# MLP of a two-layer encoder: more pairs with seven products, sums of the chunks added by DMAs, residual kept in DRAM meanwhile

## The chip, the cores and the metric

The kernel runs on one core of a Trainium2 chip. The metric is the device time of one execution in microseconds (us). The profile is one execution taken by the hardware profiler. Its engines are named PE (matrix multiplies; PEld is the load of the stationary operand, which overlaps PE), DVE (elementwise on two inputs), ACT (copies, casts, functions), POOL (elementwise, and here also an issuer of DMAs) and SP (issues DMAs only).

## The reference

256 tokens with 2048 features pass through two layers. Each layer has attention (layer 0: a chunked softmax; layer 1: stick-breaking) beside a cross-attention of four heads into 256 memory tokens, and then an MLP with 8192 hidden features. Only this part of it, and where the residual `h` is read, matter here:

```python
def sq_relu_mlp(h, g, w_in, w_out):
    return jnp.square(jax.nn.relu(rms_norm(h, g) @ w_in)) @ w_out
...
    for layer in range(DEPTH):          # DEPTH = 2
        ...
        h = h + jnp.concatenate([y_main, y_mem], axis=-1) @ w_o[layer]
        h = h + sq_relu_mlp(h, norm_mlp[layer], w_mlp_in[layer], w_mlp_out[layer])
```

Everything is float32.

## The kernel before

**Precision.** Each float32 operand is split into `hi` (a cast to the fp32r type) and `lo = x - hi`, and a product is three matmuls: hi·hi, hi·lo, lo·hi. A weight unit is 128x1024 values. SP loads it into a tile `raw` (6 buffers), ACT casts it to `hi` (4 buffers), DVE subtracts to get `lo` (5 buffers). `weights()` hands the units out in the order of a list, `stream`, and has the units after the one it hands out prepared, up to four.

**MLP.** The 8192 hidden features are four chunks `c` of 2048, and a chunk is 16 tiles `f` of 128 features. A step U computes one tile: 16 matmuls of 128x512 with the `hi` of two weight units, then 16 of 128x256 with their `lo`. Its result leaves PSUM in `up`: ACT copies one half (`low`, L449), DVE adds the other (L1174), DVE applies relu and the norm (L1156), ACT squares (L1159), and the tile is split into `hid` (L1114, L1115).

The second projection takes the tiles of a chunk in eight pairs `j`, tiles 2j and 2j+1. Its 2048 outputs are two halves `n` of 1024. For one pair and one half, tokens, features and outputs are a 2x2 by 2x2 product of blocks. It is done in one of two ways:

- directly, in two steps A and B, with one weight unit each and 12 matmuls of 128x512 each, together 24;
- with seven products instead of eight, in one step S (`seven`): 21 matmuls, from four weight units that here are called W0 to W3. W0 holds two blocks as they were loaded, W1 one block (128x512), W2 and W3 two each that DVE makes from the raw blocks in place, by four subtractions and additions of 128x512 (L220, L221 for W2; L223, L224 for W3; each needs the one before). The step uses them in this order with 6, 3, 6 and 6 matmuls. On the other side, `block_sums` makes the sums and differences of the pair's tiles, `s_w` and `s_x` (four DVE operations of 128x128, L1137 to L1140, and the splits). They serve both halves n of a chunk.

`SEVEN = 5`: pairs 0 to 4 go by S, 5 to 7 by A and B. In the last chunk only half 0 goes this way; half 1 is done plainly at the end.

**Order of the work.** `TURNS` writes out one turn per chunk and half, and `mlp_steps` reads it, both for `stream` and for the program. PE executes exactly in this order. In half 0 the turn makes the remaining U of the same chunk, in half 1 the first U of the next one. The `up` of a tile is written in the program where its U ends; the preparation of W2 and W3 of a following S is written behind it, since `weights()` looks four units ahead. The other engines' instructions are put in order by a scheduler when the kernel is built; from then on the order on each engine is fixed.

**Sums.** A turn accumulates eight PSUM banks: four outputs `11`, `21`, `12`, `22` and four products `p1`, `p5`, `p6`, `p7` that enter more than one output. `add` brings a finished bank into SBUF sums (`d`: four tiles, `e`: three, 128x1024 each). In chunk 0 these are mostly ACT copies (L1080), in later chunks DVE adds from PSUM (L1082), of which `p1` takes two. At the end `merged` adds the products into the outputs (L1027), and `turned` transposes the sums and adds them to `h` (L1011).

**Buffers.** Tiles of 128x1024 come from the pool `grp` with 13 buffers. During an MLP these hold four tiles of `h`, four `d`, three `e`, and the keys and values of the memory for layer 1.

Of the kernel before, what the change touches and what calls it, by code (L numbers as in the profile page):

```python
# [16 lines left out]
P = 128  # L17
# [28 lines left out]
SEVEN = 5  # L46
ALONE = 10
TURNS = (
    "U10 S0 U11 S1 U12 A5 S2 U13 S3 U14 A6 S4 U15 B5 B6 A7 B7",
    "U0 S0 U1 A5 U2 S1 U3 A6 U4 S2 U5 A7 U6 S3 U7 S4 U8 B5 U9 B6 B7",  # L50
)


def mlp_steps():

    steps = [(0, 0, "H", 0)] + [(0, 0, "T", f) for f in range(FIRST_UP, ALONE, 2)]
    for c in range(NCH):
        for n in range(2 if c < NCH - 1 else 1):
            for step in TURNS[n].split():
                kind, i = step[0], int(step[1:])  # L60
                steps.append((c + 1 if kind == "U" and n == 1 else c, n, kind, i))
    return steps
# [41 lines left out]
def trunk(  # L104
# [27 lines left out]
    tiny = ctx.enter_context(tc.tile_pool(name="tiny", bufs=4))  # L132
    ps_mm = ctx.enter_context(tc.tile_pool(name="ps_mm", bufs=4, space=PSUM))
# [132 lines left out]
    def start_side(g):  # L266
        active.append(g)
# [302 lines left out]
    def normed_heads(banks, eps_ms, gain, dst, wait=2):  # L570
# [24 lines left out]
        def side():  # L595
# [3 lines left out]
            for m in range(2):  # L599
# [11 lines left out]
                )  # L611

# [11 lines left out]
    def heads4(name):  # L624
        return grp.tile([P, 1024], F32, name=name, tag="g4")

# [190 lines left out]
    def mlp_stream(l):  # L817
# [5 lines left out]
        for c, n, kind, i in mlp_steps():  # L823
# [115 lines left out]
    km, vm = [], []  # L939

    for l, mg in enumerate((mg0, mg1)):
# [10 lines left out]
        def keys(b, wait, k_=k_, g=g):  # L952

            late = 2 + wait
            later(lambda: normed_heads(b, mstat["em"], sm[:, g : g + 1], k_[:], late), wait)
# [10 lines left out]
        else:  # L966
            tokens_major(mg, lambda b: keys(b, 0))
            tokens_major(mg, lambda b: value_heads(b, mstat["r"], vm[1]))
# [16 lines left out]
    def mlp(l, xg_, sq, h, done):  # L985
# [7 lines left out]
        extra = [heads4(f"e{l}_{i}") for i in range(3)]  # L993

        def product_sum(i, n):

            return extra[i][:, n * 512 : (n + 1) * 512]
# [18 lines left out]
        def merged(n):  # L1016

            u, p5, p7 = (product_sum(i, n) for i in range(3))
            for i, (dst, src) in enumerate((
                (summed(0, 2 * n + 1), u),  # L1020
                (summed(0, 2 * n + 1), p5),
                (u, p7),
                (summed(1, 2 * n), u),
                (u, p5),
                (summed(1, 2 * n + 1), u),
            )):
                pin(nc.vector.tensor_tensor(dst, dst, src, op=ALU.add))  # L1027
# [10 lines left out]
        sevens = SEVEN  # L1038

        class Group:  # L1040

            def __init__(self, c, n, factors, staged=None):
                self.c, self.factors, self.staged = c, factors, staged
# [387 lines left out]
```

## Time and profile before

| | us |
|---|---|
| runs | 2158.01, 2158.10, 2158.83 (median 2158.1) |
| profiled execution | 2158.02 |
| its span, first to last instruction | 2156.3 |
| busy: PE / DVE / ACT / POOL | 2148.9 / 1745.1 / 1248.3 / 205.5 |
| layer 0, chunk 1, half 0 | about 665 to 739 of the span |
| layer 0, chunk 1, half 1 | about 739 to 834 of the span |

Busy time is the time in which at least one instruction of the engine ran, and neighbours overlap a little; so the time that an instruction takes up in a full queue is the distance from its start to the next start, somewhat less than its own duration. "Waits" name who waited for whom. Names have their buffer numbers left out: `acc` is any PSUM accumulator. POOL issues no DMA in this kernel.

### The profile page before, as it was taken

What the parts mean: (1) busy time and instruction counts of PE and PEld (TensorE: products, weight loads), DVE (VectorE), ACT (ScalarE), POOL (GpSimd) and SP (SyncE); (2) the same over time, 40 slices, a digit from 0 to 9 for tenths busy, and PEclk for the clock granted to TensorE, in tenths of its full rate; (3) what the DMA queues carried; (4) which work ended last, traced back from release to release, by engine and by line L of the source; (5) the groups of instructions that cost most, each with busy time, mean ns of one, the idle gap of its engine ahead of it and who ended that gap; (6) DMA issues with size and microseconds to landing.
All of it is one profiled execution on the core that took longest, in us unless ns stands there. A gap on an engine that the chain in (4) does not pass through costs nothing.

```text
span 2156.3 us, 30341 instructions
## 1 busy us (share of the span) xinstructions
PE 2148.9 (100%) x11038; PEld 1841.2 (85%) x11038; DVE 1745.1 (81%) x2603; ACT 1248.3 (58%) x1828; POOL 205.5 (10%) x223
## 2 busy tenths in 40 slices
PE   9999999999999999999999999999999999999999
PEld 8888888888888888888888889888888888888887
DVE  7778885679898899989986556566988888988995
ACT  7744545556666566566555547655666656556663
POOL 0010112610000000000050112252000000000000
PEclk9999999999999999999999999999999999999999
DMA  9655556656666756666766654455666666666674
GB/s 331 193 165 187 167 180 195 196 188 187 192 200 200 214 180 197 205 199 196 215 177 194 187 187 137 131 184 184 185 214 186 197 205 200 202 194 205 186 224 128
DMA packets 213317, 414.65 MB, mean 192 GB/s; under 512 B 13232, under 2 KB 144304, under 8 KB 213168
## 3 DMA queue, kind: packets, MB, share of 16 engines
q1 hardware_dynamic: 212592, 410.63, 62.0%
q8 instruction: 86, 1.41, 0.3%
q10 hardware_dynamic: 576, 2.10, 0.3%
q14 instruction: 63, 0.52, 0.1%
HBM read 410.58 MB, written 2.10 MB: 191 GB/s over the span
## 4 chain that ended last, share of the span: by engine, by line
PE 98%; DVE 2%; issue 0%; ACT 0%; DVEq 0%
PE acc L75 93%; PE accs L75 1%; PE yp L75 1%; PE tp L75 1%; PE s L75 1%; PE z L75 1%; DVE lo L226 0%; PE cold L75 0%; DVE lo L174 0%; DVE pt L654 0%; DVE lo L248 0%; ACT hi L171 0%; DVE h L1011 0%; PE stat L75 0%; DVE raw L223 0%
## 5 line engine op out<-in xcount | busy, mean ns | idle before, releaser
L174 DVE TENSOR_TENSOR lo<-raw,hi 128x1024 fp32r<-128x1024 f32 (+1 forms) x524 | 642.5, 1237 | 220.9 <-ACT hi L171 194.8
L171 ACT CAST hi<-raw 128x1024 fp32r<-128x1024 f32 (+1 forms) x524 | 539.2, 1045 | 339.2 <-PE acc L75 286.0
L75 PE MATMUL acc<-mlpx,hi 128*128 128x512 f32 x2048 | 483.9, 389 | 0.0
L75 PE MATMUL acc<-hi,hid 128*128 128x512 f32 x1404 | 474.4, 391 | 0.0
L75 PEld LDWEIGHTS acc<-mlpx,hi 128*128 128x128 f32 x2048 | 383.6, 188 | 79.3
L225 ACT CAST hi<-raw 128x1024 fp32r<-128x1024 f32 (+1 forms) x280 | 264.8, 946 | 204.9 <-DVE raw L221 132.8
L226 DVE TENSOR_TENSOR lo<-raw,hi 128x1024 fp32r<-128x1024 f32 (+1 forms) x280 | 302.0, 1087 | 34.6 <-ACT hi L225 29.5
L75 PEld LDWEIGHTS acc<-hi,hid 128*128 128x128 f32 x1404 | 264.0, 188 | 52.6
L75 PE MATMUL acc<-lo,hid 128*128 128x512 f32 x702 | 274.5, 391 | 0.0
L75 PEld LDWEIGHTS acc<-mlpx,lo 128*128 128x128 f32 x2048 | 261.3, 191 | 9.0
L75 PE MATMUL acc<-mlpx,lo 128*128 128x256 f32 x2048 | 264.6, 283 | 0.0
L75 PE MATMUL acc<-hi,xg 128*128 128x512 f32 x640 | 208.4, 398 | 0.0
L75 PEld LDWEIGHTS acc<-lo,hid 128*128 128x128 f32 x702 | 132.3, 188 | 23.2
L247 ACT CAST hi<-raw 128x1024 fp32r<-128x1024 f32 x108 | 113.4, 1055 | 65.2 <-PE acc L75 54.6
L449 ACT COPY low<-acc 128x256 f32<-128x256 f32 x188 | 69.4, 369 | 136.1 <-PE acc L75 135.0
L75 PEld LDWEIGHTS acc<-hi,xg 128*128 128x128 f32 x640 | 120.2, 188 | 24.6
L248 DVE TENSOR_TENSOR lo<-raw,hi 128x1024 fp32r<-128x1024 f32 x108 | 131.0, 1230 | 6.1 <-ACT hi L247 6.1
L75 PE MATMUL acc<-lo,xg 128*128 128x512 f32 x320 | 124.7, 390 | 0.7 <-DVE lo L174 0.7
L75 PE MATMUL acc<-y,hi 128*128 128x512 f32 x512 | 119.9, 391 | 0.0
L75 PEld LDWEIGHTS acc<-y,hi 128*128 128x128 f32 x512 | 95.0, 188 | 19.1
L75 PE MATMUL acc<-hi,s_w 128*128 128x512 f32 x280 | 97.6, 389 | 0.0
L1159 ACT ACTIVATE up<-up 128x256 f32<-128x256 f32 x128 | 52.8, 415 | 40.2 <-DVE up L1156 40.2
(211 smaller groups left out, 2612.6 us busy)
## 6 DMA issues: line engine op xcount, KB each, us to landing
raw<-in_w_up SPq DMA_DIRECT2D x256, 512.0 KB, 4.8
raw<-in_w_down SPq DMA_DIRECT2D x256, 512.0 KB, 6.0
raw<-in_w_in SPq DMA_DIRECT2D x80, 512.0 KB, 3.9
raw<-in_w_o SPq DMA_DIRECT2D x64, 512.0 KB, 4.2
raw<-in_w_mem SPq DMA_DIRECT2D x28, 512.0 KB, 5.8
raw<-in_w_kv_v SPq DMA_DIRECT2D x24, 512.0 KB, 4.1
raw<-in_w_kv_k SPq DMA_DIRECT2D x24, 512.0 KB, 4.4
raw<-in_w_q SPq DMA_DIRECT2D x24, 512.0 KB, 4.2
```

What stands on the lines that cost most here:

```text
L75: return self._tc.keep_in_program_order(fn(*args, **kwargs))
L171: nc.scalar.copy(hi[:, :n], raw[:, :n])
L174: nc.vector.tensor_tensor(lo, raw, hi.bitcast(F32), op=ALU.subtract)
L225: nc.scalar.copy(hi4, src)
L226: nc.vector.tensor_tensor(lo4, src, hi4.bitcast(F32), op=ALU.subtract)
L247: nc.scalar.copy(hi4, turned)
L248: nc.vector.tensor_tensor(lo4, turned, hi4.bitcast(F32), op=ALU.subtract)
L449: nc.scalar.copy(low[:], bank[:, T:])
L1159: nc.scalar.activation(a[:], a[:], AF.Square)
```

## The change

The number of pairs that go by S is set by chunk: 7, 7, 6 and 5 of 8 in chunks 0 to 3, in both layers (it was 5 in each). There are new turns for 5, 6 and 7 pairs, and `ALONE` goes from 10 to 9: half 1 of a chunk makes nine U of the next, half 0 the other seven.

The bank of each output or product has one home now, so there are four `e` tiles instead of three, and `p1` is added once; `merged` makes up for it with eight adds instead of six. In chunk 0 all eight banks are copied by ACT. In chunks 1 and 2 ACT copies each bank into a half of a fresh 128x1024 tile `copy`, and when both halves are there POOL issues a DMA that adds the tile to its home in SBUF (`accum_op=ALU.add`). In chunk 3 DVE adds as before.

To make room, POOL issues DMAs that write the four tiles of `h` to DRAM as they are finished before an MLP (`put_away`) and bring them back in its last chunk (`bring_back`), and do the same with the memory keys and values of layer 1 between their computation and their use. In chunks 0 and 1 the `s_w` and `s_x` of pair 6 share a tile of `grp`.

```diff
-SEVEN = 5
-ALONE = 10
-TURNS = (
-    "U10 S0 U11 S1 U12 A5 S2 U13 S3 U14 A6 S4 U15 B5 B6 A7 B7",
-    "U0 S0 U1 A5 U2 S1 U3 A6 U4 S2 U5 A7 U6 S3 U7 S4 U8 B5 U9 B6 B7",
-)
+SEVEN = [[7, 7, 6, 5], [7, 7, 6, 5]]
+ALONE = 9
+TURNS = {
+    5: (
+        "U S0 U S1 U S2 U A5 U S3 U A6 S4 U B5 B6 A7 B7",
+        "U S0 U A5 U S1 U A6 U S2 U A7 U S3 U S4 B5 U B6 B7",
+    ),
+    6: (
+        "U S0 U S1 U S2 U S3 U S4 U A6 U S5 B6 A7 B7",
+        "U S0 U S1 U A6 U S2 U S3 U A7 U S4 U S5 U B6 B7",
+    ),
+    7: (
+        "U S0 U S1 U S2 U S3 U S4 U S5 U S6 A7 B7",
+        "U S0 U S1 U S2 U S3 U S4 U S5 U S6 U A7 U B7",
+    ),
+}
...
+    def put_away(tile_, name):
+        home = away.tile([P, 1024], F32, name=f"away_{name}", tag="away")
+        nc.gpsimd.dma_start(home[:], tile_[:])
+        return home
+
+    def bring_back(home, name):
+        tile_ = heads4(name)
+        nc.gpsimd.dma_start(tile_[:], home[:])
+        return tile_
...
-                src = self.banks[q][:]
-                if self.staged is not None and q in ("12", "22", "p1", "p5", "p6", "p7"):
-
+                src, dst = self.banks[q][:], home_of(q, self.n)
+                if self.c == 0:
+                    nc.scalar.copy(dst, src)
+                elif self.c == NCH - 1:
+                    if self.staged is None or q in ("11", "21"):
+                        nc.vector.tensor_tensor(dst, src, dst, op=ALU.add)
+                        return
                     copy = wide.tile([P, 512], F32, name="copy", tag="wide")
                     nc.scalar.copy(copy[:], src)
-                    self.staged.extend((dst, copy[:]) for dst in self.sums_of[q])
-                    return
-                for dst in self.sums_of[q]:
-                    if self.c == 0 and q not in ("11", "p6"):
-                        nc.scalar.copy(dst, src)
-                    else:
-                        nc.vector.tensor_tensor(dst, src, dst, op=ALU.add)
+                    self.staged.append((dst, copy[:]))
+                else:
+                    whole, i = place(q, self.n)
+                    first = whole.name not in self.copies
+                    if first:
+                        self.copies[whole.name] = heads4("copy")
+                    copy = self.copies[whole.name]
+                    nc.scalar.copy(copy[:, i * 512 : (i + 1) * 512], src)
+                    if not first:
+                        nc.gpsimd.dma_start(out=whole[:], in_=copy[:], accum_op=ALU.add)
...
+            if c == NCH - 1 and n == 0 and "h" not in back:
+                back["h"] = True
+                bring_h(range(3))
...
+            if o % 4 == 3:
+                h_away[o // 4] = put_away(h_tiles[o // 4], f"h{l}_{o // 4}")
...
+    km[1], vm[1] = bring_back(km_away[0], "km1b"), bring_back(vm_away[0], "vm1b")
```

The program has 60 matmuls fewer (10812 instead of 10872), 106 DVE operations more, 128 on ACT more, and 52 DMAs on POOL's queue, where there was none.

What the scheduler makes of it is seen on DVE in layer 0, chunk 1, half 1. Before, around the steps U7 and S4, which follow each other there: `lo321` to `lo324` are W0 to W3 of S4, and `up_7723` waits for the end of U7.

```order
L226 TENSOR_TENSOR lo322_7686<-raw321_1_7672,hi322_7685 128x512
L220 TENSOR_TENSOR raw321_1_7672<-raw321_1_7672 128x4x128
L221 TENSOR_TENSOR raw321_1_7672<-raw321_1_7672,raw321_0_7670 128x4x128
L223 TENSOR_TENSOR raw321_0_7670<-raw321_1_7672,raw321_0_7670 128x4x128
L224 TENSOR_TENSOR raw321_0_7670<-raw321_0_7670 128x4x128
L226 TENSOR_TENSOR lo323_7744<-raw321_1_7672,hi323_7743 128x1024
L1174 TENSOR_TENSOR up_7723<-acc_7684,low_7721 128x256
L1137 TENSOR_TENSOR s23_7729<-up_7627 128x128
L1082 TENSOR_TENSOR e0_0_4157<-acc_7093,e0_0_4157 128x512
L1082 TENSOR_TENSOR d0_1_4154<-acc_7093,d0_1_4154 128x512
L226 TENSOR_TENSOR lo324_7750<-raw321_0_7670,hi324_7749 128x1024
L1156 SCALAR_TENSOR_TENSOR up_7723<-up_7723,ri_mlp0_4388 128x256
```

After the change, around U4 and S4 of the same turn: `lo326` and `lo327` are W2 and W3 of S4, and `up_7620` waits for the end of U4. (L1228, L1210, L238 to L242 and L244 are the new numbers of L1174, L1156, L220 to L224 and L226; L1191 to L1194 of `block_sums`.)

```order
L1161 TENSOR_TENSOR s_w_7516<-s23_7514,s_w_7516 128x256
L239 TENSOR_TENSOR raw324_1_7569<-raw324_1_7569,raw324_0_7567 128x4x128
L1161 TENSOR_TENSOR s_x_7517<-s14_7515,s_x_7517 128x128
L1228 TENSOR_TENSOR up_7620<-acc_7581,low_7618 128x256
L241 TENSOR_TENSOR raw324_0_7567<-raw324_1_7569,raw324_0_7567 128x4x128
L1210 SCALAR_TENSOR_TENSOR up_7620<-up_7620,ri_mlp0_4403 128x256
L244 TENSOR_TENSOR lo326_7625<-raw324_1_7569,hi326_7624 128x1024
L242 TENSOR_TENSOR raw324_0_7567<-raw324_0_7567 128x4x128
L244 TENSOR_TENSOR lo327_7631<-raw324_0_7567,hi327_7630 128x1024
L192 TENSOR_TENSOR lo328_7644<-raw328_7642,hi328_7643 128x1024
```

Of S4's preparation only W3's `lo` stood behind the `up` before; now the arithmetic of W3 (L241, L242) and the `lo` of both W2 and W3 stand behind it.

On ACT, at the same place after the change, the copy out of U4's bank (`low_7618`) stands ahead of the casts of W2 and W3 (`hi326`, `hi327`), and the square of `up` between these.

```order
L467 COPY low_7618<-acc_7581 128x256
L243 CAST hi326_7624<-raw324_1_7569 128x1024
L1213 ACTIVATE up_7620<-up_7620 128x256
L243 CAST hi327_7630<-raw324_0_7567 128x1024
L189 CAST hi328_7643<-raw328_7642 128x1024
```

Before, both casts of S4 (`hi323`, `hi324`) stood around `low_7721` with no square between them.

On POOL, behind the last instruction ahead of the MLP of layer 0 (`root`), there are now the adding DMAs of chunk 1, four for each half.

```order
L571 TENSOR_TENSOR root_4297<-ms_4295,neg_half_122 128x4
L1128 DMA e0_0_4171<-copy_7067 128x1024
L1128 DMA e0_1_4172<-copy_7095 128x1024
L1128 DMA d0_0_4167<-copy_7123 128x1024
L1128 DMA d0_2_4169<-copy_7131 128x1024
L1128 DMA e0_2_4173<-copy_7847 128x1024
L1128 DMA e0_3_4174<-copy_7875 128x1024
L1128 DMA d0_1_4168<-copy_7970 128x1024
L1128 DMA d0_3_4170<-copy_7978 128x1024
```

Before, POOL had no instruction between `root` and the squares of the next residual.

Over the whole program, in 24 steps S of the new order, 12 in each layer, the rows between the `up` of the U just ahead and W3's `lo` read as in the second of these listings (`up`, L241, L1210, `lo` of W2, L242, `lo` of W3, in some with one `hid` before the last). In 4 more, only L242 and both `lo` stand behind the `up`. They lie in chunks 0, 1 and 2: three in each half of chunk 0, two and three in those of chunk 1, one in half 0 of chunk 2; the four others are S1 in half 0 of chunks 1 and 2. Of the 70 steps S before, none that directly followed a U had any of L220 to L224, or the `lo` of W2, behind that `up`.

131 lines of the change are left out of this document (83 added, 48 removed).

## The prediction

> I read the profile from the whole to the places that the change moves: the page first, then the waits of PE, the busy times of two turns, and the order of time around a step S.
>
> **What bounds the kernel now.** From the page: the span, the busy times, and the chain of work that ended last. Then, from the waits of PE: who waited, for whom, us in total, times, longest.
>
> ```profile
> span 2156.3 us, 30341 instructions
> PE 2148.9 (100%) x11038; PEld 1841.2 (85%) x11038; DVE 1745.1 (81%) x2603; ACT 1248.3 (58%) x1828; POOL 205.5 (10%) x223
> PE 98%; DVE 2%; issue 0%; ACT 0%; DVEq 0%
> ...
> PE tp L75 <- DVE h L1011: 2.2, 2, 1.1
> ...
> PE acc L75 <- DVE lo L174: 0.7, 1, 0.7
> ```
>
> PE is the chain, and it waits almost nowhere. A matmul less is time saved in full, and any stop of PE is time lost in full. Next, the busy time of PE, PEld, DVE, ACT, POOL in chunk 1 of layer 0, half 0 and half 1, and in the stretch that holds one of the two long waits above:
>
> ```profile
> 665.00:739.00 74.00, 74.00 (x376) 63.22 (x374) 67.53 (x87) 43.70 (x58) 0.00 (x0) 1.00 0.68 199
> 739.00:834.00 95.00, 95.00 (x491) 81.33 (x490) 85.89 (x132) 57.46 (x85) 0.00 (x0) 1.00 0.63 200
> 1077.00:1110.00 33.00, 31.88 (x153) 26.22 (x152) 29.73 (x37) 16.53 (x23) 19.70 (x20) 1.00 0.57 167
> ```
>
> The average of DVE, 81%, hides that it is 90 to 91% busy in these turns (85.89 of 95, 67.53 of 74). It is the next engine. How near it is shows the order of time around U7 and S4 of half 1 (start, us, engine, line, operands). The two long rows are U7, the others S4, up to the next U:
>
> ```profile
> 800.47 3.79 PE L75 MATMUL acc<-mlpx,hi 128*128 128x512 f32 x16
> 804.09 2.08 PE L75 MATMUL acc<-mlpx,lo 128*128 128x256 f32 x16
> 806.00 0.40 PE L75 MATMUL acc<-hi,hid 128*128 128x512 f32 x1
> ...
> 808.30 0.39 PE L75 MATMUL acc<-lo,hid 128*128 128x512 f32 x1
> ...
> 809.21 0.61 PE L75 MATMUL acc<-hi,s_w 128*128 128x512 f32 x2
> 809.75 0.50 PE L75 MATMUL acc<-lo,s_w 128*128 128x512 f32 x1
> ...
> 811.01 1.30 PE L75 MATMUL acc<-mlpx,hi 128*128 128x512 f32 x5
> ```
>
> U takes 5.53 us (800.47 to 806.00). From 806.00 to 809.21 are fourteen matmuls: 0.229 us each, so an S of 21 takes 4.81. The first matmul that needs W2's `lo` is number 11 of S (808.30, 2.30 behind S's start), and the first that needs W3's `lo` is number 17: due at 806.00 + 16 x 0.229 = 809.66, it started at 809.75. DVE at the same time:
>
> ```profile
> 802.82 0.69 DVE L220 TENSOR_TENSOR raw<-raw 128x512 f32<-128x512 f32 x1
> 803.55 0.69 DVE L221 TENSOR_TENSOR raw<-raw,raw 128x512 f32<-128x512 f32 x1
> ...
> 805.61 1.22 DVE L226 TENSOR_TENSOR lo<-raw,hi 128x1024 fp32r<-128x1024 f32 x1
> 806.74 0.42 DVE L1174 TENSOR_TENSOR up<-acc,low 128x256 f32<-128x256 f32 x1
> 807.08 0.28 DVE L1137 TENSOR_TENSOR s<-up 128x128 f32<-128x128 f32 x1
> 807.28 0.68 DVE L1082 TENSOR_TENSOR e<-acc,e 128x512 f32<-128x512 f32 x1
> 807.88 0.68 DVE L1082 TENSOR_TENSOR d<-acc,d 128x512 f32<-128x512 f32 x1
> 808.48 1.22 DVE L226 TENSOR_TENSOR lo<-raw,hi 128x1024 fp32r<-128x1024 f32 x1
> ```
>
> W3's `lo` ended at 809.70, and the matmul started 0.05 later: here PE just waits for DVE. This S is the yardstick: W3's `lo` stood behind `up`, one `s` (0.20 to the next start) and two adds (0.60 each), and that used up all that there was.
>
> **What the change removes.** 60 matmuls of 128x512, 20 steps S more with 21 instead of 24: 60 x 0.229 = 13.7 us, all on PE's chain. The DVE adds L1082 in chunks 1 and 2 go too, nine in each of eight turns, some 72 x 0.60 = 43 us of DVE.
>
> **What it adds, beside PE.** Each S in place of A and B gives DVE three `lo` of 1.13 (805.61 to 806.74), one of half size, and the four steps on the raw blocks at 0.73 (802.82 to 803.55), the last at 0.60: 3.4 + 0.6 + 2.8 = 6.8 instead of two `lo`, 2.3. That is 4.5 x 20 = 90 us; `block_sums` for ten more pairs and eight more adds in `merged` are some 20. DVE is busier by about 65 us in all, and almost all of that falls into the turns of chunks 0 and 1, which have 7 S. The evictions on ACT (64 x 0.6 = 38 us) and its casts (some 40) fit: it has 30 us free in each turn above. The DMAs are bounded by the nearest row, a load of as many bytes as one of them:
>
> ```profile
> raw<-in_w_down SPq DMA_DIRECT2D x256, 512.0 KB, 6.0
> ```
>
> One that adds may cost no more than this or some times as much (it reads two operands); even 20 us is covered, since a sum is needed again a turn later (74 us or more) and `h` comes back at the start of chunk 3 and is needed at its end. I take 0. By the Trainium skill, "DMA: Bandwidth & Descriptors", section "Anatomy of one DMA — SWDGE (gpsimd) path", a DMA issued by GpSimd takes about 2.0 us plus its bytes over 436 GB/s, an estimate of 3.2 us here; no run here shows one, and the sum would be the same. The write of `h` sits between two squares on POOL, ahead of each MLP, with a U's worth of matmuls before its result is due: 0 to 1 us, I take 0.
>
> **What it adds on PE's chain.** In the new turns U and S alternate without an A between, and in the fixed order of DVE 24 steps S have more than the yardstick behind the `up` of the U that ends as S starts: `up`, L241, L1210, W2's `lo`, L242, W3's `lo`. How soon `up` can start, and what these take, shows another place, where S's U ended at 710.35 (the first PE row; an A follows there, which is why it cost nothing):
>
> ```profile
> 710.35 0.40 PE L75 MATMUL acc<-hi,hid 128*128 128x512 f32 x1
> ...
> 710.54 0.37 ACT L449 COPY low<-acc 128x256 f32<-128x256 f32 x1 [3.10 <-PE acc L75]
> ...
> 710.95 0.42 DVE L1174 TENSOR_TENSOR up<-acc,low 128x256 f32<-128x256 f32 x1
> 711.29 0.68 DVE L224 TENSOR_TENSOR raw<-raw 128x512 f32<-128x512 f32 x1
> 711.89 0.42 DVE L1156 SCALAR_TENSOR_TENSOR up<-up,ri_mlp 128x256 f32<-128x256 f32 x1
> 712.23 1.22 DVE L226 TENSOR_TENSOR lo<-raw,hi 128x1024 fp32r<-128x1024 f32 x1
> ```
>
> `up` starts 0.60 behind the end of U: it waits for ACT's copy, and everything behind it on DVE waits with it, ready or not. Then 0.34 (`up`), 0.60 (L241), 0.34 (L1210): W2's `lo` starts at 1.88 and ends at 3.10. PE wants it at 2.30: a first stop of about 0.9. L242 starts at 3.01. W3 must now be cast after it, and only then comes its `lo`; that trip is here:
>
> ```profile
> 775.70 0.69 DVE L224 TENSOR_TENSOR raw<-raw 128x512 f32<-128x512 f32 x1
> 776.31 2.48 DVE L226 TENSOR_TENSOR lo<-raw,hi 128x1024 fp32r<-128x1024 f32 x2
> 776.48 1.05 ACT L225 CAST hi<-raw 128x1024 fp32r<-128x1024 f32 x1 [0.41 <-DVE raw L224]
> ```
>
> The cast starts 0.78 behind L224 and takes 1.05, and the second `lo` in the second row starts at 776.31 + 2.48 - 1.22 = 777.57, so 1.87 behind L224. In the new order: 3.01 + 1.87 = 4.88, ended at 6.10, matmul 17 at 6.15. It is due at 16 x 0.229 = 3.66. The stop is 2.5 us in both parts, per such S. The yardstick gives the same from the other side: behind its `up` stood 1.40 us, here 0.60 + 0.34 + 1.13 + 1.87 = 3.94, and it had no slack: 2.54 later. A later start of `up` (the yardstick's came 0.74 behind U's end) adds to it.
>
> Does DVE arrive in time for that? Between two such `up` lie two U and two S. From the even `up`: 0.34 + 0.60 + 0.34 + 1.13 + 1.87 + 1.13, then four `lo` (4.0), four raw steps (2.8), a `lo` (1.1): 13.3. From the odd one: `up`, four `lo`, one of half size, `block_sums` and its splits, two raw steps: some 9.1. Together 22.4. PE needs 2 x (5.53 + 4.81) = 20.7 without a stop and 23.2 with one. So DVE is just in time once PE has stopped, and without the unlucky order it would still fall behind by up to 1.7 us in each pair of U and S.
>
> In four more S only L242 and both `lo` stand behind `up`: W2's `lo` is late as above by 0.9, W3's then about in time. 24 x 2.5 + 4 x 0.9 = 63.6 us.
>
> Small terms, taken at 0: the first S of chunk 0, whose U comes one U earlier (the work of `block_sums` ahead of it is spread over the same matmuls but one U's 5.5 us; 0 to 3); `h`'s last tile, which may land late at the end of layer 1 (0 to 3); the adds in `merged`, whose turns at the end have room on DVE.
>
> **The sum**, against the profiled execution, 2158.02 us (its span and 1.7 around it; 0.1 below the median of the runs): 2158.0 - 13.7 + 63.6 = 2208. Changes under 0.2%, 4 us, I count as none.
>
> **Rivals.** (1) DVE keeps ahead and PE never stops: 2158.0 - 13.7 = 2144, faster. For it speaks that PE waited for a weight only 0.7 us by name in the whole trace, with DVE at 90%; against it the yardstick, where a shorter row of work left nothing. It needs all of L241, L1210, W2's `lo`, L242 and the cast within 3.0 us of U's end, and they take 4.9; it wins if the stops average under 0.35 us (28 x 0.35 = 10 of the 13.7, less the 4).
> (2) Only DVE's total counts, because its waits at `up` are shorter than I think: up to 1.7 us lost for each of 28 places, less a lead of about 2 us in each of ten turns: 0 to 28, so 2144 to 2172, middle 2158: no change or slightly slower.
> (3) PE slows after each stop. If the rest of such an S (five matmuls) ran at half pace, 24 x 5 x 0.23 = 28 more: 2236. Against it: in the stretch 1077 to 1110, with one of PE's two long waits (up to 1.1 us), the granted clock is 1.00. The Trainium skill, "TensorE: Matmul & The Clock Gate", section "A second HAM failure mode: psum-queue depth-cycling", says that frequent short idles of PE between groups of matmuls make the clock gate drop to half and come back; with its window of 3.4 us that would be 24 x 1.7, an estimate of 41 us more, so 2249. The trace shows no drop, but no series of stops either.
> (4) DVE falls further behind, so that the odd S stop too, by 0.5 to 1 us at some twenty places: 2220 to 2230.
>
> **How the numbers follow.** My forecast, 2195 to 2219 (stops of 2.0 to 2.9 us at the 24 places), 0.70; (4) 0.10; (3) 0.04; (2) 0.09; (1) 0.07. Predicted: 2208. For the range I leave out (1), (3) and the lower half of (2), some 0.16: 2175 to 2230. Faster by more than 0.2%: (1) and a little of (2), 0.08. Within 0.2%: 0.04 of (2). Slower: 0.88.
>
> **What the new profile would show.** Right: PE about 60 us of idle time, in stops of about 0.9 and 1.6 us, put down to DVE's `lo` L244, at S1, S3, S5 of half 0 and S2, S4, S6 of half 1 in chunks 0 and 1, and hardly any in chunk 3; DVE's `up` L1228 at 0.60 behind a U's end there; half 1 of chunk 1 longer than before although it has fewer matmuls; DVE busy about 1810 us. Wrong: PE busy throughout and the span near 2143; stops at matmuls that wait for `copy`, a DMA or a PSUM bank; or a granted clock below 1.00. The prediction falls if DVE runs L241 and W2's `lo` before the `up` that stands ahead of them.

## The result, and the profile after

The changed kernel takes 2249.29 us (median of 5 runs, 2247.23 to 2254.64) against 2158.1 before: a ratio of 1.0425, 95% interval 1.041 to 1.0439, slower by 91 us. The prediction was 2208, with a range of 2175 to 2230: the direction is right, the size is not, and the time lies outside the range. From the page after: span, busy times, and the chain by engine and by line.

```profile
span 2247.4 us, 30605 instructions
...
PE 2171.9 (97%) x10978; PEld 1831.2 (81%) x10978; DVE 1792.6 (80%) x2709; ACT 1311.9 (58%) x1956; POOL 241.4 (11%) x275
...
PE 84%; DVE 8%; DMA 3%; ACT 3%; issue 1%; SPq 0%; ACTq 0%
```

PE was 98% of the chain and is 84%; DVE went from 2% to 8%, and ACT and also DMA have entered it. What PE waited for (us in total, times, longest):

```profile
PE acc L92 <- DVE lo L244: 42.7, 57, 1.5
PE acc L92 <- ACT hi L243: 11.3, 26, 2.7
PE acc L92 <- ACT hid L1160: 10.3, 5, 2.3
```

The first row is the wait that was forecast. The third was not, and the second is larger than forecast. First the forecast place, S4 in half 1 of chunk 0, layer 0 (PE and DVE in order of time; a row ends with the idle time ahead of it):

```profile
624.21 2.08 PE L92 MATMUL acc<-mlpx,lo 128*128 128x256 f32 x16
...
626.72 0.42 DVE L1228 TENSOR_TENSOR up<-acc,low 128x256 f32<-128x256 f32 x1 [0.72 <-ACT low L467]
627.07 0.68 DVE L241 TENSOR_TENSOR raw<-raw,raw 128x512 f32<-128x512 f32 x1
627.66 0.42 DVE L1210 SCALAR_TENSOR_TENSOR up<-up,ri_mlp 128x256 f32<-128x256 f32 x1
628.00 1.22 DVE L244 TENSOR_TENSOR lo<-raw,hi 128x1024 fp32r<-128x1024 f32 x1
629.14 0.68 DVE L242 TENSOR_TENSOR raw<-raw 128x512 f32<-128x512 f32 x1
630.93 1.22 DVE L244 TENSOR_TENSOR lo<-raw,hi 128x1024 fp32r<-128x1024 f32 x1 [1.11 <-ACT hi L243]
...
629.27 0.50 PE L92 MATMUL acc<-lo,hid 128*128 128x512 f32 x1 [0.70 <-DVE lo L244]
...
630.95 0.50 PE L92 MATMUL acc<-hi,s_w 128*128 128x512 f32 x1 [0.26 <-ACT hi L243]
...
632.21 0.50 PE L92 MATMUL acc<-lo,s_w 128*128 128x512 f32 x1 [0.76 <-DVE lo L244]
```

U ends at 626.12, `up` starts 0.60 behind it and holds everything behind it. W2's `lo` ends 3.10 behind U's end and W3's `lo` starts 4.81 behind it, where 3.10 and 4.88 were forecast. DVE idles 0.72 + 1.11 = 1.83 us in it.

To see what each place costs, the distance from the start of each matmul to the next was taken from the trace, less the usual one of its shape (0.228 us for 512 columns, 0.120 for 256), and added up by step of the program. That gives the table on which the rest rests. Its columns: the 24 steps S of the forecast; S1 in half 0 of chunks 1 and 2, the 4 other ones; A7 and B7 of half 0 in chunks 0 and 1, with A7 of chunk 3; S0 and S1 of chunk 3 with the U behind S1; the rest of both MLPs (from rounding alone it stands near -2). Of the 24 steps, e2_five has 16 and e13_six 20. "Time" is the median of the runs; the other columns are of the profiled execution, which lies up to 4 us beside it (2244.35 in e4_bring). The kernel before, run again beside each of these kernels, took 2158.55 to 2158.91. What each kernel is follows below.

| kernel | time | 24 S | 4 S | A7, B7 | S0, S1 of c3 | rest |
|---|---|---|---|---|---|---|
| before | 2158.1 | 0.5 | 0.0 | -0.2 | -0.1 | -1.9 |
| after | 2249.3 | 61.7 | 5.6 | 20.8 | 12.9 | 0.4 |
| e1_pin | 2212.5 | 18.8 | 4.8 | 23.6 | 13.6 | 4.2 |
| e2_five | 2182.9 | 5.1 | 4.8 | 1.8 | 14.7 | -3.3 |
| e4_bring | 2240.3 | 61.6 | 5.7 | 23.0 | 2.6 | 3.1 |
| e5_square | 2243.1 | 61.7 | 5.0 | -0.2 | 14.6 | 10.1 |
| e6_apart | 2215.0 | 61.7 | 4.0 | -0.2 | 0.0 | -2.9 |
| e7_all | 2174.6 | 18.8 | 3.1 | -0.2 | 0.0 | 0.9 |
| e8_all_pool | 2188.6 | 33.3 | 3.4 | -0.2 | 1.3 | -1.8 |
| e9_polo | 2190.4 | 35.0 | 4.7 | -0.2 | 0.0 | -2.1 |
| e10_noc3 | 2186.2 | 33.3 | 4.7 | 1.8 | 0.1 | -2.2 |
| e11_skiplo | 2149.5 | 0.8 | 0.0 | -0.2 | 0.1 | -3.1 |
| e12_plain | 2230.7 | 61.6 | 4.0 | 19.0 | 0.0 | -2.9 |
| e13_six | 2162.6 | 6.3 | 3.1 | 1.8 | 0.0 | -2.1 |
| e14_late | 2187.4 | 27.5 | 3.6 | 2.3 | 1.3 | 5.1 |

In the row of after the 24 places hold 61.7 us (2.57 each, all between 2.55 and 2.58), where 60 were forecast, and the four others 5.6, where 3.6 were. Of the 91.1 us between the two spans, -13.7 + 61.2 + 5.6 = 53 were forecast in kind. The other 38 are A7 and B7 (21), the start of chunk 3 (13), and 4 in small pieces.

**A7.** The last tile of a chunk, 15, has only S6 between its U and its first use. In chunk 0, layer 0, U ended at 561.45; DVE, then ACT, then PE:

```profile
564.14 0.42 DVE L1210 SCALAR_TENSOR_TENSOR up<-up,ri_mlp 128x256 f32<-128x256 f32 x1
...
563.34 2.00 ACT L265 CAST hi<-raw 128x1024 fp32r<-128x1024 f32 x2
565.24 1.08 ACT L1112 COPY e<-acc 128x512 f32<-128x512 f32 x2
566.19 1.07 ACT L189 CAST hi<-raw 128x1024 fp32r<-128x1024 f32 x1
567.14 0.44 ACT L1213 ACTIVATE up<-up 128x256 f32<-128x256 f32 x1
...
567.92 1.08 ACT L189 CAST hi<-raw 128x1024 fp32r<-128x1024 f32 x1
568.87 0.44 ACT L1160 CAST hid<-up 128x256 fp32r<-128x256 f32 x1
...
569.35 0.50 PE L92 MATMUL acc<-hi,hid 128*128 128x512 f32 x1 [2.28 <-ACT hid L1160]
...
572.36 0.63 PE L92 MATMUL acc<-lo,hid 128*128 128x512 f32 x1
```

The tile was ready for its square at 564.5. On ACT the square stands behind two casts, two copies out of PSUM (new at this place with the change) and another cast, and comes 2.6 us later; the `hid` cast waits again. So the square starts 5.69 behind U's end. In the kernel before, U of the same tile ended at 554.09, and nothing stood ahead of its square on ACT, which came 1.64 behind:

```profile
555.73 0.42 ACT L1159 ACTIVATE up<-up 128x256 f32<-128x256 f32 x1 [1.07 <-DVE up L1156]
```

And after the stop the matmuls are slow (0.63 in the row at 572.36 above instead of 0.39). The stretches 566 to 571 and 571 to 576 (us, busy PE, PEld, DVE, ACT, POOL, granted clock, DMA share, GB/s):

```profile
566.00:571.00 5.00, 2.17 (x9) 1.18 (x8) 3.62 (x4) 3.30 (x6) 0.00 (x0) 1.00 0.88 246
571.00:576.00 5.00, 5.00 (x16) 3.93 (x15) 0.99 (x1) 2.59 (x4) 0.00 (x0) 0.66 0.81 288
```

**Chunk 3.** The loads for S1 in layer 0 were issued at 1027.42 and their first cast could start at 1046.19; the first matmul of S1 that needs W2 is the last row:

```profile
1027.42 1.85 SPq L226 DMA_DIRECT2D raw<-in_w_down  x2
...
1046.19 1.05 ACT L243 CAST hi<-raw 128x1024 fp32r<-128x1024 f32 x1 [4.02 <-DMA raw<-in_w_down]
...
1053.73 0.79 PE L92 MATMUL acc<-hi,s_x 128*128 128x512 f32 x1 [2.67 <-ACT hi L243]
```

The two loads took 18.7 and 19.9 us from issue to landing, where the median is 6. In that time POOL's last four adding DMAs and three tiles of `h` were under way. The DMA share of the stretches, and from the page's DMA issues (KB each, median us to landing):

```profile
1020.00:1030.00 10.00, 10.00 (x54) 8.57 (x53) 9.25 (x14) 8.26 (x15) 1.69 (x2) 1.00 0.90 223
1030.00:1040.00 10.00, 10.00 (x53) 8.47 (x51) 6.57 (x9) 5.50 (x9) 2.86 (x4) 1.00 1.06 318
...
raw<-in_w_down SPq DMA_DIRECT2D x256, 512.0 KB, 6.1
...
e<-copy POOLq DMA_DIRECT2D x16, 512.0 KB, 10.7
d<-copy POOLq DMA_DIRECT2D x16, 512.0 KB, 8.7
hb<-away_h POOLq DMA_DIRECT2D x8, 512.0 KB, 7.2
```

The DMA engines are full there (share 1.06; it was 0.60 from 1000 to 1020).

### The profile page after: what moved, and what is told of

It is laid out like the page before. It is cut to its first block, busy times and chain, and to the rows that moved or that the text cites. A ratio compares the mean times of both kernels' runs of the same rounds, so it can differ in the third digit from the quotient of the medians.

```text
span 2247.4 us, 30605 instructions
## 1 busy us (share of the span) xinstructions
PE 2171.9 (97%) x10978; PEld 1831.2 (81%) x10978; DVE 1792.6 (80%) x2709; ACT 1311.9 (58%) x1956; POOL 241.4 (11%) x275
## 3 DMA queue, kind: packets, MB, share of 16 engines
q0 software_dynamic: 7488, 27.27, 5.0%
## 4 chain that ended last, share of the span: by engine, by line
PE 84%; DVE 8%; DMA 3%; ACT 3%; issue 1%; SPq 0%; ACTq 0%
PE acc L92 80%; DVE lo L244 3%; DMA raw<-in_w_down 3%; ACT hi L243 1%; PE yp L92 1%; PE accs L92 1%; DVE raw L242 1%; DVE raw L241 1%; PE tp L92 1%; PE s L92 1%; PE z L92 1%; DVE up L1228 1%; ACT hi L189 0%; ACT low L467 0%; DVE lo L192 0%
## 5 line engine op out<-in xcount | busy, mean ns | idle before, releaser
L192 DVE TENSOR_TENSOR lo<-raw,hi 128x1024 fp32r<-128x1024 f32 (+1 forms) x524 | 639.7, 1237 | 194.4 <-ACT hi L189 169.9
L189 ACT CAST hi<-raw 128x1024 fp32r<-128x1024 f32 (+1 forms) x524 | 537.5, 1044 | 289.7 <-PE acc L92 235.1
L243 ACT CAST hi<-raw 128x1024 fp32r<-128x1024 f32 x360 | 338.6, 944 | 257.8 <-DVE raw L239 156.3
L244 DVE TENSOR_TENSOR lo<-raw,hi 128x1024 fp32r<-128x1024 f32 x360 | 387.9, 1086 | 99.1 <-ACT hi L243 94.9
L92 PE MATMUL acc<-hi,hid 128*128 128x512 f32 x1244 | 439.2, 396 | 12.3 <-ACT hid L1160 10.3
L92 PEld LDWEIGHTS acc<-hi,hid 128*128 128x128 f32 x1244 | 236.9, 191 | 62.6 <-ACT hid L1160 12.4
L92 PE MATMUL acc<-lo,hid 128*128 128x512 f32 x622 | 249.4, 401 | 22.5 <-DVE lo L244 22.5
L92 PEld LDWEIGHTS acc<-lo,hid 128*128 128x128 f32 x622 | 118.9, 191 | 55.8 <-DVE lo L244 36.3
L92 PE MATMUL acc<-hi,s_w 128*128 128x512 f32 x328 | 122.2, 403 | 5.0 <-ACT hi L243 5.0
L1128 POOL DMA_DIRECT2D e<-copy x16 | 13.8, 863 | 1047.2 <-ACT copy L1126 745.7
L265 ACT CAST hi<-raw 128x1024 fp32r<-128x1024 f32 x68 | 71.1, 1057 | 42.3 <-PE acc L92 33.9
L266 DVE TENSOR_TENSOR lo<-raw,hi 128x1024 fp32r<-128x1024 f32 x68 | 83.4, 1240 | 12.9 <-ACT hi L265 12.6
```

Source lines behind the costliest of these rows:

```text
L92: return self._tc.keep_in_program_order(fn(*args, **kwargs))
L189: nc.scalar.copy(hi[:, :n], raw[:, :n])
L192: nc.vector.tensor_tensor(lo, raw, hi.bitcast(F32), op=ALU.subtract)
L243: nc.scalar.copy(hi4, src)
L244: nc.vector.tensor_tensor(lo4, src, hi4.bitcast(F32), op=ALU.subtract)
L265: nc.scalar.copy(hi4, turned)
```

## The experiments

**e1_pin: the order alone.** The theory of the prediction put to the test: only the order on DVE is changed.

```diff
-        elif seven.step == 2:
-            nc.vector.tensor_tensor(b22, b22, b12, op=ALU.subtract)
-            nc.vector.tensor_tensor(b12, b12, b11, op=ALU.subtract)
-        elif seven.step == 3:
-            nc.vector.tensor_tensor(b11, b22, b11, op=ALU.add)
-            nc.vector.tensor_tensor(b21, b21, b11, op=ALU.subtract)
         nc.scalar.copy(hi4, src)
         nc.vector.tensor_tensor(lo4, src, hi4.bitcast(F32), op=ALU.subtract)
+        if seven.step == 1:
+            nc.vector.tensor_tensor(b22, b22, b12, op=ALU.subtract)
+            nc.vector.tensor_tensor(b12, b12, b11, op=ALU.subtract)
+            nc.vector.tensor_tensor(b11, b22, b11, op=ALU.add)
+            nc.vector.tensor_tensor(b21, b21, b11, op=ALU.subtract)
...
-            nc.vector.tensor_tensor(t[:], bank[:, :T], low[:], op=ALU.add)
+            pin(nc.vector.tensor_tensor(t[:], bank[:, :T], low[:], op=ALU.add), not early)
```

> The changed kernel with another order on DVE: all four raw steps of an S (L238 to L242 of the changed kernel) are written right behind the lo of its W1, and the up of a tile is kept behind them. So only up, lo of W2, the relu step and lo of W3 stand behind the end of a U, with the cast of W3 free to run earlier. In the changed kernel each of the 24 steps S stops PE for 2.57 us (0.86 + 0.11 + 0.42 + 1.03 + 0.11), and DVE idles 0.72 + 1.11 in it. Theory (the order is the cause): up starts about 0.5 later than now, W2's lo ends about 0.4 behind its due time and W3's lo about 0.1: 0.5 to 0.8 a stop instead of 2.57, 24 x 1.9 = 45 us less, 2204 (2195 to 2215). Rival (the order is a symptom, DVE's later work grows by what is saved): DVE works 21.4 us in each period of 23.2 that PE could do in 20.7, so at least 0.7 a pair stays in any order; if DVE cannot use the 1.83 us that it idles, less than 15 us are gained: above 2234. Second rival (PE stops for another reason, such as the loads): 2249, no change.

2212.45 us. The 24 stops fell from 2.57 to 0.78 each, all alike. DVE at the same S4, with L242 and L243 as the last two raw steps and L1227 as `up` in this kernel:

```profile
618.87 0.69 DVE L242 TENSOR_TENSOR raw<-raw,raw 128x512 f32<-128x512 f32 x1
619.60 0.69 DVE L243 TENSOR_TENSOR raw<-raw 128x512 f32<-128x512 f32 x1
620.21 0.42 DVE L1227 TENSOR_TENSOR up<-acc,low 128x256 f32<-128x256 f32 x1
620.63 1.23 DVE L238 TENSOR_TENSOR lo<-raw,hi 128x1024 fp32r<-128x1024 f32 x1
621.77 0.42 DVE L1209 SCALAR_TENSOR_TENSOR up<-up,ri_mlp 128x256 f32<-128x256 f32 x1
622.11 1.22 DVE L238 TENSOR_TENSOR lo<-raw,hi 128x1024 fp32r<-128x1024 f32 x1
```

No idle time of DVE is left in these rows. The order was the cause of 43 of the 61.7 us; 37 showed in the time, since A7, B7 and the rest grew by 7.

**e2_five: the DMAs without the pairs.** `SEVEN` is 5 in all chunks; the sums, the copies and the put-away tensors stay as changed.

```diff
-SEVEN = [[7, 7, 6, 5], [7, 7, 6, 5]]
+SEVEN = [[5, 5, 5, 5], [5, 5, 5, 5]]
```

> The changed kernel with 5 of 8 pairs by S in every chunk, as before the change; what stays of the change is the adding DMAs, the copies on ACT, the put-away tensors and the nine U in half 1. Theory (the DMAs are not free: weight loads that are in flight with them land late): the stop at S1 of the last chunk, 6.9 us in layer 0 and 5.9 in layer 1, stays, and little else: 2158 + 13 = 2171 (2164 to 2180). Rival (the term of the DMAs is zero as forecast, and all the stops come from the seventh and sixth pairs): 2158 (2154 to 2162). Second rival (the evictions on ACT delay the last tile of a chunk too): 2171 + up to 18 = 2189.

2182.9 us, 25 more than before with the same matmuls, above the range of the first theory and below the second rival. The start of chunk 3 holds 14.7 of them (13 expected). The other 11.7 by the table, which the theory missed, are S1 in half 0 of chunks 0 to 2, with stops of the same kind as in the changed kernel (0.86, 0.41 and 1.03 in chunk 0), and one A7.

**e4_bring: the three tiles of `h` later and apart.** A copy of one column, which waits for a tile of `hid`, goes ahead of each DMA on POOL.

```diff
+            nc.gpsimd.tensor_copy(tile_[:, :1], behind)
             nc.gpsimd.dma_start(tile_[:], home[:])
...
-                bring_h(range(3))
+            late = {("S", 2): (0, 11), ("A", 5): (1, 12), ("S", 3): (2, 13)}.get((kind, i))
+            if c == NCH - 1 and n == 0 and late:
+                bring_h([late[0]], hid[:, late[1], :1].bitcast(F32))
```

> The changed kernel with the first three tiles of h brought back later and apart: each DMA is made to wait for one of the tiles hid 11, 12 and 13 of the last chunk, so one of them in about ten us, behind the last adding DMAs. Theory (three tiles of h and the last adding DMAs together hold up the loads of S1 of the last chunk, which landed 19 to 20 us after their issue instead of 4 to 6): the stops of 6.9 and 5.9 us go, 2249 - 12.8 = 2236.5 (2232 to 2240). Rival (the two last adding DMAs alone do it): more than half of it stays, 2243 to 2249. Second rival (each tile brought back later holds up a load by itself): the stop moves to a later S and the time stays at 2249.

2240.3: the start of chunk 3 fell from 12.9 to 2.6, as the first theory has it. The rest and A7 took 5 back, most of the former at S1 of chunk 2, half 1 (3.5 and 2.3 us).

**e5_square: tile 15 ahead.** The cast and `lo` of B7's weights and the copies out of PSUM are queued behind the splits of tile 15.

```diff
+            if stream[i].last:      # B7 of half 0
+                queued(cast, "hi")  # behind the hi of hid 15
+                queued(rest, "lo")  # behind its lo
...
-                    nc.scalar.copy(dst, src)
+                    queued(nc.scalar.copy(dst, src), "hi")
```

> The changed kernel with the last tile of a chunk (tile 15) put ahead on ACT and DVE: the cast of B7's weights, the copies out of the PSUM banks and B7's lo are queued behind the splits of that tile. Theory (A7 waits 4 to 4.6 us for tile 15 in half 0 of chunks 0 and 1 because its square and its split stand on ACT behind two casts, the copies of finished banks and a cast for the next U, and the matmuls after a stop of 2.4 run at 0.43 us each): about 17 of the 18.6 us lost there go, 2232 (2227 to 2238). Rival (DVE's relu step, which stands behind W3's lo, is already too late): about half stays, 2240. Second rival (the casts and copies that are now behind it are late in turn, at B7 or in the first U of the next half): no gain, 2245 to 2250.

A7 and B7 lost all of their 20.8 us, as the theory has it, and yet only 6 showed: 2243.05. The rest grew by 10, nearly all of it at S1 of chunk 1, half 1 (5.9 and 3.8 us), and 4.7 came up outside of the two MLPs' steps, 2.9 of it a transpose at the end that waits for a sum. SP, ACT and PE there:

```profile
750.66 1.88 SPq L227 DMA_DIRECT2D raw<-in_w_down  x2
...
767.57 1.05 ACT L244 CAST hi<-raw 128x1024 fp32r<-128x1024 f32 x1 [6.15 <-DMA raw<-in_w_down]
...
768.67 0.50 PE L92 MATMUL acc<-hi,hid 128*128 128x512 f32 x1 [0.40 <-ACT hi L244]
```

A load was 17 us under way, beside four adding DMAs that POOL issued within six microseconds. In the changed kernel two loads at this place took as long (18.2 us), and PE did not wait for them: the stop at A7 had given them the time that they needed. Once it was gone, the DMAs showed.

**e6_apart: e5_square with the DMAs set apart.** Each adding DMA waits for another tile of `hid` of the next turn; the tiles of `h` come behind the last of them.

```diff
-                        nc.gpsimd.dma_start(out=whole[:], in_=copy[:], accum_op=ALU.add)
+                        pending.append((whole, copy))
...
+            if pending and written["tile"] != written["last"]:
+                add_one()   # a copy of one column of that tile, then the DMA
```

> The kernel e5_square (tile 15 put ahead) with its DMAs set apart: each adding DMA of chunks 1 and 2 waits for another tile of hid of the next turn, so that one is issued in 10 to 20 us instead of four in about 10, and the first three tiles of h come back behind the last of them, apart too. Theory (loads that are in flight with several of POOL's DMAs land late; in e5_square that took back 5.9 and 3.8 us at S1 of chunk 1, half 1, and 7.1 and 6.6 at S1 of chunk 3): those 23 us go but for about 1 us each that other kernels show at S1: 2243 - 20 = 2223 (2217 to 2228); the 24 stops of 2.57 stay. Rival (each adding DMA holds up a load by itself, in steps without slack): the stops spread over more steps and the time stays above 2237.

2214.95, 28 less, 8 better than expected: no step of the turns but the 28 forecast ones stops by more than 0.3 us. The same adding DMAs, bytes and sums stop PE nowhere when they are issued 7 to 34 us apart.

**e7_all: the three edits together** (the diffs of e1_pin, e5_square and e6_apart).

> The three edits together: the order on DVE of e1_pin, tile 15 ahead of e5_square, the DMAs apart of e6_apart. By the steps: e1_pin 2212.5, less its stops at A7 and B7 (23.6), at U8 (1.9) and at S1 of chunk 3 (12.4): 2175 (2168 to 2183), with 24 stops of 0.78 left. Rival (DVE, which works 21.4 us a pair of U and S against 20.7 on PE, has used the stops to catch up): each stop that goes makes the next ones longer, 2185 to 2200.

2174.6 against 2175: the pieces add up. Only the 28 stops of 0.78 (W2's `lo`) and three at U8 are left.

**e11_skiplo: less work for DVE.** e7_all with another `split` for the pairs that go by S; it leaves out `x - hi`:

```diff
+            if skip:
+                nc.scalar.copy(hi, src)
+                nc.scalar.copy(lo, src)
+                return
```

> e7_all with part of DVE's work left out: the lo of hid, s_w and s_x of the pairs that go by S in chunks 0 to 2 is not x - hi but a second copy on ACT (so the low part of these operands is wrong). DVE's work for two U and two S falls by 1.2 us to 20.2, PE's is 20.7, and POOL does nothing beside it. Theory (what e7_all has left, 24 stops of 0.78 and three at U8, 22 us in all, is that DVE has more to do in these turns than PE): they go, 2174.6 - 21 = 2153 (2149 to 2159). Rival (the stops come from up and the cast, a round trip that stays): 24 x 0.5 stay, 2166 or more.

2149.5 (ratio to before 0.9958, 0.9945 to 0.9972): every stop in the turns is gone. The stretch 560 to 670 of e7_all, and then of this kernel:

```profile
560.00:670.00 110.00, 108.50 (x548) 91.15 (x547) 100.20 (x145) 75.76 (x114) 0.00 (x0) 1.00 0.66 201
```

```profile
560.00:670.00 110.00, 110.00 (x568) 94.26 (x567) 99.38 (x136) 82.45 (x136) 0.00 (x0) 1.00 0.68 204
```

PE is busy throughout, and does 20 matmuls more in the same time. So what e1_pin and e7_all have left is DVE's total: two U and two S took 20.7 + 2.57 = 23.2 us in the changed kernel, 1.83 of which DVE idled. That leaves 21.4 us of work for DVE against 20.7 on PE, and the difference, 0.7, is the stop.

**e8_all_pool, e9_polo, e10_noc3, e14_late: the same relief by POOL.** e8_all_pool gives POOL the four sums of `block_sums`, e9_polo instead the `lo` of `hid`, `s_w` and `s_x`. e10_noc3 is e9_polo with tile 15 put ahead in chunks 0 to 2 only. e14_late is e8_all_pool with the splits of `s_w` and `s_x` later on DVE.

```diff
-            nc.vector.tensor_tensor(s23[:, P:], a11, a21, op=ALU.subtract)
+            nc.gpsimd.tensor_tensor(s23[:, P:], a11, a21, op=ALU.subtract)      # e8, e14: and three more
...
+            engine = nc.gpsimd if pool else nc.vector                           # e9, e10
...
+                later(lambda: [pin(split(*home)[1]) for home in homes[1:]], 7)  # e14
```

> e7_all with the four sums of block_sums (128x128, 0.20 each on DVE) done by POOL: DVE's work for two U and two S falls from 21.4 to 20.6 us, below PE's 20.7. Theory (what is left of the 24 stops, 0.78 each, is DVE's load): the stops nearly vanish, e7_all less 24 x 0.6 = 14, so about 2160 (2152 to 2168). Rival (POOL's four dependent sums of 0.6 or more each make s_w and s_x late, or slow DVE beside them): S waits for s_w instead, no better than e7_all.

> e7_all with the lo of hid, s_w and s_x (x - hi, for the pairs that go by S in chunks 0 to 2) made by POOL instead of DVE; the sums of block_sums stay on DVE, so DVE waits for nothing of POOL's. DVE's work for two U and two S falls by 2 x 0.34 + 0.34 + 0.20 = 1.2 us, from 21.4 to 20.2, below PE's 20.7. Theory (what e7_all has left, 24 stops of 0.78 and three at U8, is DVE's load): they go, 2174.6 - 21 = 2153 (2147 to 2162), at last below the kernel before. Rival (as in e8_all_pool, POOL's longer way makes something late, here hid or s_w for the matmuls): 2170 or above. Second rival (DVE beside a busy POOL is slower): the stops shrink by half, 2164.

> e9_polo, with tile 15 put ahead in chunks 0 to 2 only, and in the last chunk the order of the change. In e7_all a transpose at the end of layer 1 waits 2.9 us for a sum of DVE, which the change does not have, while the change waits 2.0 at A7 of that chunk. Theory (the tile that is put ahead there pushes the sums back): 1 us less than e9_polo. Rival (the transpose waits for the late return of h): no difference.

> e8_all_pool (the four sums of block_sums on POOL) with the splits of s_w and s_x written a U and an S later, and kept on DVE behind the lo of the weights there, so that DVE no longer stands behind POOL's chain with the raw steps of the next S in line; tile 15 is put ahead in chunks 0 to 2 only. Theory (DVE's load, 20.6 us for two U and two S against PE's 20.7, is all that was left; e8_all_pool lost by the order): no stop above 0.2 in the turns with 7 S, e7_all 2174.6 less 22 and less the 2 to 4 that e10_noc3 stood below e9_polo: 2150 (2146 to 2157), below the kernel before. Rival (DVE is slower beside POOL, as in e9_polo, where raw steps took 1.11 instead of 0.69): stops of about 0.5 to 1 stay in each pair, 2163 to 2185.

2188.6, 2190.4, 2186.2 and 2187.4: 12 to 16 us slower than e7_all, each time against the theory. e10_noc3 gained 4.2 on e9_polo, where 1 was expected. In the two profiled executions, which are 2.7 apart, the transpose's wait of 2.9 is gone, A7 of chunk 3 stops for 2.0 again, and 1.7 is a drop of PE's clock that e9_polo has at one S1 (shown in the next section); so the edit itself gave 0.9. Rows of e9_polo (a `lo` on POOL, two raw steps on DVE), then of e14_late (two sums on POOL, the `hid` of DVE that waits, and the cast on ACT that it waits for):

```profile
612.14 3.95 POOL L1181 TENSOR_TENSOR hid<-up,hid 128x256 fp32r<-128x256 f32 x1 [14.02 <-ACT hid L1180]
...
593.87 1.11 DVE L243 TENSOR_TENSOR raw<-raw,raw 128x512 f32<-128x512 f32 x1
595.02 1.11 DVE L244 TENSOR_TENSOR raw<-raw 128x512 f32<-128x512 f32 x1
```

```profile
610.52 3.42 POOL L1212 TENSOR_TENSOR up<-up 128x128 f32<-128x128 f32 x1 [9.31 <-ACT up L1241]
...
614.02 0.46 POOL L1213 TENSOR_TENSOR s<-up 128x128 f32<-128x128 f32 x1
614.41 0.42 DVE L1180 TENSOR_TENSOR hid<-up,hid 128x256 fp32r<-128x256 f32 x1 [0.79 <-ACT hid L1179]
...
613.98 0.41 ACT L1179 CAST hid<-up 128x256 fp32r<-128x256 f32 x1 [2.63 <-POOL up L1212]
```

The same kind of sum takes POOL 0.46 or 3.42 us, and a raw step takes DVE 1.11 instead of 0.69: the two engines hold each other up. The Trainium skill, "SBUF — State Buffer", section "Who interferes with whom", says that a DVE instruction with two inputs in SBUF contends with a GpSimd instruction that reads SBUF, over shared ports that are locked for one of the two. The rows agree: POOL's 3.42 us lie beside DVE instructions that follow each other without a gap (609.20 to 613.62), its 0.46 in the 0.79 us in which DVE waits. In the turns of e9_polo no instruction of DVE or ACT waits for POOL, so there the slowing is all that is left: in the stretch 560 to 670 DVE is busy 101.0 us with 131 instructions, where e7_all has 100.2 with 145. In e14_late the cast that DVE's `hid` needs waits for POOL as well (the last row), so its order still put DVE behind POOL's chain, and what of the loss in e8_all_pool and e14_late is that and what is the slowing was not separated.

**e12_plain: DMAs that only write.** The call without `accum_op`.

> The changed kernel with its DMAs to the sums only writing (the copy overwrites the sum instead of being added, so the sums lack chunks). Theory (loads in flight with POOL's DMAs land late because of the bytes that all move, adding or not): a DMA to a sum takes somewhat less than its 9 to 11 us, weight loads at the starts of the turns still land 10 us and more after their issue, and the time stays within 8 us of 2249. Rival (the adding is what is slow and holds up the loads): these DMAs land in 4 to 6 us, the loads too, S1 of chunk 3 stops for 1 to 2 us instead of 6.9 and 5.9, about 2238.

2230.7 (2 runs): the theory that the bytes alone do it is wrong, since the time fell by 18.6 us where it allowed 8, and the start of chunk 3 lost all of its 12.9. The rival is right that the adding matters, but not in its figures: these DMAs land in 6.6 to 8.5 us, not in 4 to 6. The DMA issues, and the stretch 1030 to 1040:

```profile
e<-copy POOLq DMA_DIRECT2D x16, 512.0 KB, 8.5
d<-copy POOLq DMA_DIRECT2D x16, 512.0 KB, 6.6
...
1030.00:1040.00 10.00, 10.00 (x53) 8.62 (x52) 8.78 (x13) 6.51 (x9) 1.58 (x3) 1.00 1.04 388
```

At the same DMA share (1.04 and 1.06) 388 GB/s are moved instead of 318: adding takes up time of the DMA engines in which less is moved. Over the whole span POOL's queue takes 5.0% of the engines' time with the adding and 3.1% without it, for the same 27.27 MB. The loads beside it were late still (13.6 and 14.5 us), but not enough to stop PE. So either relief ends the stop at the start of chunk 3, the tiles of `h` later (e4_bring) or no adding; in chunk 1 of e5_square the adding DMAs made a stop without any tile of `h`.

**e13_six: fewer pairs with the right order.** e7_all with 6, 6, 6 and 5 pairs (tile 15 put ahead in chunks 0 to 2).

```diff
-SEVEN = [[7, 7, 6, 5], [7, 7, 6, 5]]
+SEVEN = [[6, 6, 6, 5], [6, 6, 6, 5]]
```

> The three edits of e7_all (tile 15 ahead in chunks 0 to 2 only) with 6, 6, 6 and 5 pairs by S instead of 7, 7, 6 and 5: 36 matmuls fewer than before the change instead of 60. Theory (DVE's load, step by step): A and B between the S let DVE catch up, so in half 1 no stop is left and in half 0 two of 0.78 in each of chunks 0 to 2, 9.4 us in all; 2158.1 - 8.2 + 9.4 + 2 = 2161 (2155 to 2168), better than 7, 7, 6 and 5 though it saves less. Rival (each S more pays, once the order is right): the 24 matmuls more make it 5.5 slower than e7_all, 2176 to 2180.

2162.6, ratio to before 1.0018 (1.0009 to 1.0027): 12 us better than e7_all though it has 24 matmuls more, with 12 stops of 0.78 instead of 28. It is the best version that leaves no work out, and it does not beat the kernel before (4 us slower). Only e11_skiplo does, which leaves work out.

## Why the prediction was wrong, point by point

- **PE bounds, and a stop is time lost in full**: right. The times follow the sums of the stops, but for up to 5 us outside of the turns.
- **24 stops of 2.5 us by the order on DVE**: right in place, mechanism and size: 2.57 at each of the 24, in the two parts foretold (0.86 + 0.11, then 0.42 + 1.03 + 0.11; 0.9 and 1.6 were written). e1_pin shows that the order is the cause, and not only beside it.
- **4 more of 0.9**: 1.0 in chunk 1, 1.8 in chunk 2; the latter fell to 1.0 in e6_apart and e12_plain, so 0.8 of it is late loads.
- **"Without the unlucky order it would still fall behind by up to 1.7 us in each pair"**: right in kind; 0.78 (e1_pin, e7_all), and zero with 1.2 us less for DVE (e11_skiplo). The 22.4 us of DVE's work per pair were 21.4.
- **The DMAs at 0**: the first step that failed. I asked how soon the sum and `h` are needed, and for that the 8.7 to 10.7 us are indeed covered. I did not ask what the DMAs do to those in flight beside them. In the changed kernel the term measured 12.9 us at the start of chunk 3 (10.3 of them go with e4_bring, all with e12_plain) and some 5 elsewhere (against e6_apart, 1.6 in the 4 S and 3.3 in the rest); 10 more were hidden behind A7's stop (e5_square). With that stop out of the way, setting the DMAs apart gave 28 us (e5_square to e6_apart).
- **The evictions on ACT "fit: it has 30 us free in each turn"**: the second step that failed. Free time in a turn says nothing about one instruction that is due. The square of tile 15 stood behind work that was due later, and that cost 20.8 us in five places. The same view that I used for DVE, what stands behind what, was not used for ACT.
- **Rival (3), PE slows after each stop**: not at the 24 places, where three stops in a row (0.86, 0.42, 1.03 in 3.8 us) leave the granted clock at 1.00 (stretch 600 to 660). The estimate worked out there from the Trainium skill, "TensorE: Matmul & The Clock Gate", section "A second HAM failure mode: psum-queue depth-cycling", was 2249, which is by chance the measured time; the drops that it priced do not come at these stops. They come elsewhere: after 2.28 + 0.56 us of waiting at A7 the granted clock was 0.66 on average over 5 us. How long PE waits does not settle it alone. In e9_polo PE waits 1.00 and then 0.95 us at S1 of chunk 0 in both layers; the clock holds in layer 0 (first row, from 506) and drops in layer 1 (second row, from 1550):

```profile
506.00:511.00 5.00, 4.05 (x17) 3.01 (x17) 5.00 (x7) 4.72 (x6) 0.00 (x0) 1.00 0.45 154
1550.00:1555.00 5.00, 4.05 (x11) 3.01 (x11) 5.00 (x6) 4.30 (x5) 0.00 (x0) 0.66 0.45 147
```

  What decides it stays open. The mean clock of the changed kernel's execution, 0.995, makes the drops 0.005 x 2247 = 11 us in all, most of them in the 20.8 and the 12.9.
- **Rival (4), the odd S stop too**: did not happen.
- **What the new profile would show**: `up` at 0.60 behind U's end and a longer half 1 of chunk 1 (96.7 us after 96.0) came; DVE is busy 1793 us, not 1810. Chunk 3 has stops, where hardly any were forecast, and two of the signs of being wrong came too: PE waits behind a late DMA there, and the mean clock is below 1.00.
- **The range** stopped at 2230, since I had summed what the terms that I saw could be, and had given none to the two I set to 0.

## What to carry to other kernels

Where an instruction on the path waits for an engine that executes in a fixed order, the question is not how much free time that engine has but what stands ahead of the one row that is due, and it has to be asked of every engine that the change gives work to. A DMA that is not needed for long still takes its share of the engines that the urgent loads go through: four in six microseconds nearly tripled the landing time of loads that PE needed (6 to 17 us in e5_square), the same four spread over a turn stopped PE nowhere. A stop that is taken away can uncover the next one behind it, so its gain is read from the steps and not from the total.

## What the runs showed of the hardware

- A DMA that adds 512 KB in SBUF landed in 8.7 to 10.7 us where several were in flight (medians in the changed kernel) and in 6.2 to 8.8 when they were set apart (e6_apart); one that only writes in 6.6 to 8.5 (e12_plain). Weight loads in flight with several adding ones landed in 9 to 20 us instead of 4 to 6. The Trainium skill, "DMA: Bandwidth & Descriptors", section "Queues, rings and completion order", says that each DMA engine takes its queues in turn; loads of SP's queue that slow down as POOL's queue has work agree with that.
- PE's granted clock fell to 0.66 on average over 5 us after a wait of 2.28 us followed by 0.56, and after 1.00 followed by 0.95 in one place of e9_polo but not in another; it held through 0.86, 0.42 and 1.03 at 24 places.
- POOL and DVE on operands in SBUF slowed each other: 0.46 to 3.42 us for the same kind of sum on POOL (e14_late), 0.69 to 1.11 us for a raw step on DVE (e9_polo).
